# Turns between blocks: ScalarE writes the rounded input itself, and the splits of later weights are moved behind the turning of x

## The chip, the cores and the metric

The kernel runs on one core of one Trainium2 chip. The metric is the device time of that core in microseconds (us). Before the change the median of 3 runs is 1807.88 us (1806.29 to 1808.33). The engines are called PE (matmul; PEld is its weight load), DVE (VectorE), ACT (ScalarE), POOL (GpSimd) and SP (its queue issues most transfers).

## The reference, cut to what matters

A stack of four blocks (gated linear attention, a spatial gating unit, forgetting attention, gated linear attention again) on 256 tokens of 1024 features, followed by a hybrid block (convolution and dilated attention) and a mixture of 16,384 single-vector experts. What matters here is what lies between two blocks:

```
for i in range(DEPTH):                        # 4 blocks
    mod = cond @ w_mod[i] + b_mod[i]          # shift, scale, gate
    h = rms_norm(x, norm_pre_g[i]) * (1.0 + scale) + shift
    o = mixer_i(h)                            # begins with h @ w_in, ends with @ w_out
    x = x + gate * rms_norm(o, norm_post_g[i])
h = x + hybrid_mixer(rms_norm_2(x, norm_mix), ...)
h = h + peer_ffn(rms_norm_2(h, norm_ffn), ...)
return rms_norm_2(h, final_norm)
```

Everything is float32, and the results must hold to nearly that accuracy.

## The kernel before, in words

**Products in three parts.** Every large product a @ w is made of three matmuls in the rounded format fp32r: both operands are split into a high half (the value rounded to fp32r, suffix H or `wh`) and a low half (what the rounding left, suffix L or `wl`), and aH·wh, aH·wl and aL·wh are added up (L420 to L422). A chunk of a weight is 128 x 1024 numbers; `w_load` (L191) brings it in through SP's queue, `w_split` lets ACT write the high half (L200) and DVE the low half (L201), and asks for the load of the chunk four places later. Four raw and six split chunks are kept at a time. `w_next` hands out the next chunk and splits ahead of it; `w_fill(n)` splits all chunks up to number n-1.

**A turn.** x lies with tokens on partitions, and the next block needs h with features on partitions. A turn between two blocks works on the two halves of the tokens, tb = 0 and 1, in turn. The last group of columns of the output product (`proj_tm` with `late`) does its four chunks first for tb 0 and then for tb 1. After tb 0, `consume` takes the sums (square on ACT L348, product with the gate on DVE L484), and `late(0)` works out the norm (L355 to L500), the new x (L505) and the normed x in two pieces of 512 columns, `xn` (L361 in `scaled`). When tb 1's matmuls have been issued, `settle` turns xn of tb 0 with eight PE transposes (L367), and `make_h` works on the result: per 128 features one ACT instruction writes scaled and shifted h (L385, or L383 where there is no shift), and per pair of these DVE copies the rounded high half (L388) and subtracts for the low half (L389). Then `late(1)` begins the same for tb 1, whose turning falls into the first group of the next block (`proj_tm` with `early`), between that group's four chunks for tb 0 and its four for tb 1. There are five such turns: into sgu, fox, the second gla, the hybrid block and the experts' query (L1194 to L1204 work on its result). The first gla has an early group without a turn before it.

**Order.** The kernel is scheduled by hand: each engine runs its instructions in the order in which the program emits them. The table `FILL` tells after which chunk of the first (tb 0) and of the second pass (tb 1) further weights are split. Let `first` be the number of the first chunk of the group. Before the pass begins, chunks up to first+4 are split already. In the late group `w_fill(first+6)` therefore splits one chunk in the first pass, and `w_fill(first+7)` and `w_fill(first+8)` one each after the first and second chunk of the second pass. In the early group that follows, chunks e+0 to e+3 are its own (e = first+4), and its fills split e+4 and e+5 in the first pass and e+6 and e+7 in the second. `consume` comes before `settle` in both passes.

**Beside it.** Generators in `tasks` and `later` advance one step at each `tick`. One of them, `mod_steps`, runs beside each of the four blocks and adds up one chunk of `w_mod` per tick on DVE (L252, L254) for the modulation of later blocks, and asks SP for the chunk after the next (`m_load`, L237). In both gla blocks a long row of DVE work (`decay`, `k_scale`) has to be done before the scores (L652) can begin.

Of the kernel before, what the change touches and what calls it, by code (L numbers as in the profile page):

```python
# [8 lines left out]
F32 = mybir.dt.float32  # L9
# [3 lines left out]
AF = mybir.ActivationFunctionType  # L13
ALU = mybir.AluOpType
# [11 lines left out]
RAW = 4  # L26
HIGH = 6
LEAD = 5
FILL = ((5, 6, 0, 0), (7, 8, 0, 0))
PJ = 3  # L30
RAW2 = 3
HIGH2 = 3
# [29 lines left out]
def _build(ctx, nc, tc, I, out, dbg):  # L62
# [14 lines left out]
    act = nc.scalar.activation  # L77
    tt = nc.vector.tensor_tensor
    ts = nc.vector.tensor_scalar
# [3 lines left out]
    def pj():  # L83
        return ps_j.tile([P, 512], F32, tag="pj", name="pj")
# [13 lines left out]
    def tick():  # L98
        for g in list(tasks):
            try:  # L100
                next(g)
            except StopIteration:
                tasks.remove(g)
        tick_later()
# [5 lines left out]
    def tick_later():  # L110
        for g in list(later):
            try:
                next(g)
            except StopIteration:
                later.remove(g)
        return bool(later)
# [4 lines left out]
    x = keep.tile([P, NTB, D], F32, name="x")  # L121
# [31 lines left out]
    for l in range(4):  # L153
        if l in (0, 3):
            j = l // 3
# [37 lines left out]
    def w_split(i):  # L193
        if i >= len(plan):
            return
        w = raw.pop(i)
        pool = spool if i < first_down else late_pool[0]
        wh = pool.tile([P, CH], F32R, tag="wh", name="wh")
        wl = pool.tile([P, CH], F32R, tag="wl", name="wl")
        act(wh, w, AF.Copy)  # L200
        tt(wl, w, wh.bitcast(F32), op=ALU.subtract)  # L201
        a = plan[i][1]
        parts[i] = (wh.rearrange("p (a b) -> p a b", a=a), wl.rearrange("p (a b) -> p a b", a=a))
        w_load(i + RAW)

    def w_fill(n):
        while nxt_s[0] < n:
            nxt_s[0] += 1
            w_split(nxt_s[0] - 1)

    def w_next(fill=True):
        i = nxt_w[0]
        nxt_w[0] += 1
        if fill:
            w_fill(min(i + LEAD + 1, max(i, first_down) + HIGH2))
        return parts.pop(i)
# [113 lines left out]
    def advance():  # L330

        for g in list(pend):
            if next(g):
                pend.remove(g)
                turning.append(g)

    def settle():
        while pend:
            advance()
        while turning:  # L340
            for _ in turning.pop(0):
                pass

    HALF = [slice(m * 512, (m + 1) * 512) for m in range(2)]
# [12 lines left out]

    def scaled(tb, r):
        xn = [work.tile([P, 512], F32, tag="xn", name="xn", bufs=2) for _ in range(2)]
        for m in range(2):  # L360
            ts(xn[m], x[:, tb, HALF[m]], r, None, op0=ALU.mult)  # L361
        return xn

    def turned(xn):
        p = pm()
        for j in range(4):
            nc.tensor.transpose(p[:, j * P:(j + 1) * P], xn[:, j * P:(j + 1) * P], ident)  # L367
        return p.rearrange("p (j t) -> p j t", j=4)

    def make_h(tb, r, A, B, hs):  # L370

        h, hH, hL = hs
        tsl = slice(tb * P, (tb + 1) * P)
        xn = scaled(tb, r)
        yield True
        ps = [turned(v) for v in xn]
        for m, p in enumerate(ps):
            k4 = slice(4 * m, 4 * m + 4)
            t = h[:, k4, tsl] if h is not None else work.tile([P, 4, P], F32, tag="tl", name="tl", bufs=2)
            for j in range(4):  # L380
                kt = 4 * m + j
                if B is None:
                    act(t[:, j], p[:, j], AF.Copy, scale=A[:, kt:kt + 1])  # L383
                else:
                    act(t[:, j], p[:, j], AF.Identity, scale=A[:, kt:kt + 1], bias=B[:, kt:kt + 1])  # L385
                if j % 2:
                    e = slice(kt - 1, kt + 1)
                    nc.vector.tensor_copy(hH[:, e, tsl], t[:, j - 1:j + 1])  # L388
                    tt(hL[:, e, tsl], t[:, j - 1:j + 1], hH[:, e, tsl].bitcast(F32), op=ALU.subtract)  # L389

    def proj_fm(n, H, L, consume, nk=KT, per_block=False):

# [19 lines left out]
    def proj_tm(n, H, L, consume, early=False, late=None):  # L412


        def part(p, w, c, tb):
            wh, wl = w
            tsl = slice(tb * P, (tb + 1) * P)
            for k in range(2):
                kt = c * 2 + k
                mm(p, H[:, kt, tsl], wh[:, k], start=(kt == 0), stop=False)  # L420
                mm(p, H[:, kt, tsl], wl[:, k], start=False, stop=False)  # L421
                mm(p, L[:, kt, tsl], wh[:, k], start=False, stop=(kt == KT - 1))  # L422

        for gi in range(n):
            if early and gi == 0 or late is not None and gi == n - 1:
                first = nxt_w[0]
                ws = []
                p = pj()
                for c in range(4):
                    ws.append(w_next(False))  # L430
                    part(p, ws[c], c, 0)
                    advance()
                    if FILL[0][c]:
                        w_fill(first + FILL[0][c])
                consume(gi, 0, p)
                settle()
                if late is not None:
                    pend.append(late(0))
                    advance()
                p = pj()  # L440
                for c in range(4):
                    part(p, ws[c], c, 1)
                    advance()
                    if FILL[1][c]:
                        w_fill(first + FILL[1][c])
                    tick()
                consume(gi, 1, p)
                if late is not None:
                    settle()
                    pend.append(late(1))  # L450
                    advance()
                continue
            ps = [pj() for _ in range(NTB)]
            for c in range(4):
                w = w_next()
                for tb in range(NTB):
                    part(ps[tb], w, c, tb)
                if c == 3:
                    for tb in range(NTB):
                        consume(gi, tb, ps[tb])  # L460
                tick()

    def out_proj(oH, oL, lp, tags, l, A, B, full):
# [30 lines left out]
        def late(tb):  # L494
            r = inv_rms(ss[tb], "a")
            products(1, tb)
            c = tiny.tile([P, 2], F32, tag="c", name="c")
            tt(c, ss[tb][:, 2:6:2], ss[tb][:, 3:6:2], op=ALU.add)
            stt(c[:, 0:1], c[:, 0:1], r, c[:, 1:2], op0=ALU.mult, op1=ALU.add)
            stt(ms[tb], c[:, 0:1], r, ms[tb], op0=ALU.mult, op1=ALU.add)  # L500
            r2 = power(ms[tb], 1, "b")
            yield
            for m in range(2):
                xv = x[:, tb, HALF[m]]
                stt(xv, t[tb][:, HALF[m]], r, xv, op0=ALU.mult, op1=ALU.add)  # L505
            yield from make_h(tb, r2, A(), B(), hs)

        add(gate())
        proj_tm(2, oH, oL, consume, late=late)
        return hs  # L510

# [43 lines left out]
    def gla(l, hs, lp, nA, nB, nF):  # L555
# [63 lines left out]
        def c_v(g, tb, p):  # L619
            if tb == 1:  # L620
                act(v[:, tb, g * 512:(g + 1) * 512], p, AF.Copy)
            else:
                nc.vector.tensor_copy(v[:, tb, g * 512:(g + 1) * 512], p)  # L623

        proj_tm(2, hH, hL, c_v, early=True)

        def c_q(c, p):
# [86 lines left out]
    def sgu(l, hs, lp, nA, nB, nF):  # L714
# [19 lines left out]

        add(mod_steps([1] * 24), later)
        proj_tm(2, hH, hL, c_v, early=True)

        def ln():
# [193 lines left out]
    def hybrid(hs):  # L932
        h, hH, hL = hs
        with tc.tile_pool(name="hyb", bufs=1) as lp:
# [216 lines left out]
            def late(tb):  # L1151
                r = inv_rms(ss[tb], "b")
                yield
                yield from make_h(tb, r, col("norm_ffn", 0, 8), None, hs2)
# [317 lines left out]
    h, hH, hL = hs  # L1472

    def start():
        ss = [tiny.tile([P, 2], F32, tag=f"ss{tb}", name="ss") for tb in range(NTB)]
        for tb in range(NTB):
            for m in range(2):
                square_sum(x[:, tb, HALF[m]], ss[tb][:, m:m + 1])
        yield
        r = [inv_rms(ss[tb], "b", ms[tb]) for tb in range(NTB)]  # L1480
        yield
        for tb in range(NTB):
            xn = scaled(tb, r[tb])
            yield
            for m in range(2):
                d = h[:, 4 * m:4 * m + 4, tb * P:(tb + 1) * P]
                if m:
                    nc.vector.tensor_copy(d, turned(xn[m]))
                else:
                    act(d, turned(xn[m]), AF.Copy)  # L1490
# [155 lines left out]
```

## Time and profile before

| | |
|---|---|
| median of 3 runs | 1807.88 us |
| the profiled execution's own time | 1805.22 us |
| its span | 1803.3 us |
| PE busy (share of the span) | 1689.9 us (94%) |
| DVE busy | 1285.0 us (71%) |
| ACT busy | 970.6 us (54%) |
| chain that ended last, by engine | PE 74%, DVE 13%, ACT 5%, DMA 4%, issue 3% |
| mean granted clock of the core, as a share of full speed | 0.978 |

All rows come from the one profiled execution. A busy time counts an instruction from start to end; where instructions overlap, a row with several (x8) gives the time from the first start to the last end. "idle before" is the engine's idle time just before a group, and the releaser is what ended it.

### The profile page before, as it was taken

How to read it: one execution, taken by the hardware profiler on the slowest of the kernel's cores; microseconds unless marked ns; L12 is line 12 of the kernel's file. 1: busy time of each engine (PE TensorE's matmuls, PEld its weight loads, DVE VectorE, ACT ScalarE, POOL GpSimd, SP SyncE). 2: the span in 40 equal slices, each digit the busy share in tenths (PEclk: the TensorE clock that was granted, in tenths of full speed). 3: DMA queues.
4: the chain of work that ended last, by engine and by line, in shares of the span. 5: the costliest groups of instructions: out<-in, count | busy, mean ns of one | idle time of the engine just before them, and what ended most of it. 6: DMA issues, size and time to landing. Idle time of an engine off the chain costs nothing.

```text
span 1803.3 us, 28515 instructions
## 1 busy us (share of the span) xinstructions
PE 1689.9 (94%) x10774; PEld 1491.9 (83%) x10774; DVE 1285.0 (71%) x2593; ACT 970.6 (54%) x1527; POOL 62.1 (3%) x102
## 2 busy tenths in 40 slices
PE   3989899999989999989988999999999899999997
PEld 2877787777789788879978999999999788888886
DVE  7878787876786756574566889997774466666665
ACT  3535446545545543435353446668894455555554
POOL 0000000000000000000000000000000000000000
PEclk9989999999989999999999999999999899999999
DMA  8765885862553565335553676664447677777774
GB/s 332 268 221 177 294 285 177 314 214 71 169 190 115 190 181 174 114 95 173 170 173 117 203 220 192 204 184 158 156 150 233 199 232 238 236 236 236 236 234 159
DMA packets 104188, 357.08 MB, mean 198 GB/s; under 512 B 12273, under 2 KB 13297, under 8 KB 103794
## 3 DMA queue, kind: packets, MB, share of 16 engines
q1 hardware_dynamic: 97200, 335.52, 58.9%
q0 software_dynamic: 5120, 16.78, 2.4%
q10 hardware_dynamic: 1730, 2.96, 0.5%
q8 instruction: 85, 1.39, 0.3%
q14 instruction: 53, 0.43, 0.1%
HBM read 337.38 MB, written 17.83 MB: 197 GB/s over the span
## 4 chain that ended last, share of the span: by engine, by line
PE 74%; DVE 13%; ACT 5%; DMA 4%; issue 3%; POOL 0%; SPq 0%; DVEq 0%; ACTq 0%; POOLq 0%
PE pm L1433 20%; PE pj L1382 6%; PE pj L1383 6%; PE pj L1381 6%; PE pj L420 5%; PE pj L421 4%; PE pj L422 4%; DVE wl L201 4%; PE pj L403 4%; PE pj L404 4%; PE pj L405 4%; DMA wmod<-in_w_mod 3%; PE pm L1324 3%; DVE macc L254 2%; ACT wh L200 1%
## 5 line engine op out<-in xcount | busy, mean ns | idle before, releaser
L201 DVE TENSOR_TENSOR wl<-wr,wh 128x1024 fp32r<-128x1024 f32 x504 | 613.8, 1222 | 313.8 <-ACT wh L200 312.9
L200 ACT ACTIVATE wh<-wr 128x1024 fp32r<-128x1024 f32 x504 | 527.2, 1054 | 223.3 <-PE pm L1433 52.2
L1381 PE MATMUL pj<-uH,wh 128*128 128x256 f32 x1024 | 293.7, 287 | 0.0
L1382 PE MATMUL pj<-uH,wl 128*128 128x256 f32 x1024 | 289.9, 283 | 0.0
L1383 PE MATMUL pj<-uL,wh 128*128 128x256 f32 x1024 | 289.9, 283 | 0.0
L403 PE MATMUL pj<-hH,wh 128*128 128x256 f32 x768 | 227.0, 296 | 0.3 <-DVE v L623 0.3
L404 PE MATMUL pj<-hH,wl 128*128 128x256 f32 x768 | 221.9, 289 | 2.5 <-DVE wl L201 2.5
L405 PE MATMUL pj<-hL,wh 128*128 128x256 f32 x768 | 221.0, 288 | 0.0
L1382 PEld LDWEIGHTS pj<-uH,wl 128*128 128x128 f32 x1024 | 196.4, 192 | 0.3 <-DVE wl L201 0.2
L1381 PEld LDWEIGHTS pj<-uH,wh 128*128 128x128 f32 x1024 | 196.6, 192 | 0.0
L1383 PEld LDWEIGHTS pj<-uL,wh 128*128 128x128 f32 x1024 | 196.2, 192 | 0.0
L1433 PE MATMUL pm<-wh 128*128 128x512 f32 x512 | 161.6, 397 | 8.1 <-ACT wh L321 8.1
L420 PE MATMUL pj<-wh,hH 128*128 128x512 f32 x352 | 145.1, 412 | 21.0 <-DVE hH L388 16.3
L1433 PE MATMUL pm<-wh,wl 128*128 128x512 f32 x512 | 161.3, 396 | 0.0
L1433 PE MATMUL pm<-wl,wh 128*128 128x512 f32 x512 | 161.3, 396 | 0.0
L403 PEld LDWEIGHTS pj<-hH,wh 128*128 128x128 f32 x768 | 151.6, 197 | 11.5 <-issue 8.3
L404 PEld LDWEIGHTS pj<-hH,wl 128*128 128x128 f32 x768 | 151.8, 198 | 3.4 <-DVE wl L201 3.2
L405 PEld LDWEIGHTS pj<-hL,wh 128*128 128x128 f32 x768 | 151.5, 197 | 0.0
L422 PE MATMUL pj<-wh,hL 128*128 128x512 f32 x352 | 141.7, 403 | 0.3 <-DVE hL L1513 0.3
L421 PE MATMUL pj<-wl,hH 128*128 128x512 f32 x352 | 141.5, 402 | 0.0
L1433 PEld LDWEIGHTS pm<-wh 128*128 128x128 f32 x512 | 97.0, 190 | 31.0 <-ACT wh L321 8.3
L254 DVE SCALAR_TENSOR_TENSOR macc<-wmod,sc,macc 128x1024 f32<-128x1024 f32 x76 | 97.2, 1278 | 32.1 <-DMA wmod<-in_w_mod 31.9
(337 smaller groups left out, 2678.4 us busy)
## 6 DMA issues: line engine op xcount, KB each, us to landing
wr<-in_down SPq DMA_DIRECT2D x128, 512.0 KB, 3.7
wr<-in_up SPq DMA_DIRECT2D x128, 512.0 KB, 4.3
wmod<-in_w_mod SPq DMA_DIRECT2D x88, 512.0 KB, 5.5
wr<-in_hyb_fm SPq DMA_DIRECT2D x40, 512.0 KB, 3.6
wr<-in_hyb_qkv SPq DMA_DIRECT2D x36, 512.0 KB, 3.7
spill<-st POOLq DMA_DIRECT2D x64, 256.0 KB, 3.3
a<-spill SPq DMA_DIRECT2D x64, 256.0 KB, 3.3
wr<-in_fox_qkv SPq DMA_DIRECT2D x24, 512.0 KB, 4.3
```

What stands on the lines that cost most here:

```text
L200: act(wh, w, AF.Copy)
L201: tt(wl, w, wh.bitcast(F32), op=ALU.subtract)
L403: mm(o, wh[:, kt, cs], H[:, kt], start=(kt == 0), stop=False)
L404: mm(o, wl[:, kt, cs], H[:, kt], start=False, stop=False)
L405: mm(o, wh[:, kt, cs], L[:, kt], start=False, stop=(kt == nk - 1))
L420: mm(p, H[:, kt, tsl], wh[:, k], start=(kt == 0), stop=False)
L421: mm(p, H[:, kt, tsl], wl[:, k], start=False, stop=False)
L422: mm(p, L[:, kt, tsl], wh[:, k], start=False, stop=(kt == KT - 1))
L1381: mm(o, wh[:, kt], uH[:, kt], start=(kt == 0), stop=False)
L1382: mm(o, wl[:, kt], uH[:, kt], start=False, stop=False)
L1383: mm(o, wh[:, kt], uL[:, kt], start=False, stop=(kt == KT - 1))
L1433: mm(acc[tb][n], lw[:, m, tsl], ru[:, 0, HALF[n]], start=(i == 0 and lw is wh and ru is uh), stop=(i == P - 1 and lw is wl))
```

## The change

It has four parts. (1) In `scaled` the second of the two pieces of xn is written by ACT. (2) In `make_h` ACT writes the rounded half of each pair of features directly from the turned x, two instructions, and then the unrounded h, two more; DVE's copy is gone and its subtraction stays. (3) `FILL` becomes a table for early and late groups: the late group splits first+5 and first+6 in its passes and first+7 only after `late(1)` has been begun ("end"); the early group splits nothing in its first pass and one chunk after each chunk of the second. (4) `settle` comes before `consume` in both passes.

```diff
-FILL = ((5, 6, 0, 0), (7, 8, 0, 0))
+FILL = {"early": ((0, 0, 0, 0), (5, 6, 7, 8)), "late": ((5, 6, 0, 0), (7, 0, 0, 0)), "end": 8}
...
     def scaled(tb, r):
         xn = [work.tile([P, 512], F32, tag="xn", name="xn", bufs=2) for _ in range(2)]
-        for m in range(2):
-            ts(xn[m], x[:, tb, HALF[m]], r, None, op0=ALU.mult)
+        ts(xn[0], x[:, tb, HALF[0]], r, None, op0=ALU.mult)
+        act(xn[1], x[:, tb, HALF[1]], AF.Copy, scale=r[:, 0:1])
         return xn
...
-            for j in range(4):
+            for j in (0, 2):
                 kt = 4 * m + j
-                if B is None:
-                    act(t[:, j], p[:, j], AF.Copy, scale=A[:, kt:kt + 1])
-                else:
-                    act(t[:, j], p[:, j], AF.Identity, scale=A[:, kt:kt + 1], bias=B[:, kt:kt + 1])
-                if j % 2:
-                    e = slice(kt - 1, kt + 1)
-                    nc.vector.tensor_copy(hH[:, e, tsl], t[:, j - 1:j + 1])
-                    tt(hL[:, e, tsl], t[:, j - 1:j + 1], hH[:, e, tsl].bitcast(F32), op=ALU.subtract)
+                e = slice(kt, kt + 2)
+                for d in (hH[:, e, tsl], t[:, j:j + 2]):
+                    for i in range(2):
+                        k = kt + i
+                        if B is None:
+                            act(d[:, i], p[:, j + i], AF.Copy, scale=A[:, k:k + 1])
+                        else:
+                            act(d[:, i], p[:, j + i], AF.Identity, scale=A[:, k:k + 1], bias=B[:, k:k + 1])
+                tt(hL[:, e, tsl], t[:, j:j + 2], hH[:, e, tsl].bitcast(F32), op=ALU.subtract)
...
             if early and gi == 0 or late is not None and gi == n - 1:
                 first = nxt_w[0]
+                last = late is not None and gi == n - 1
+                fill = FILL["late" if last else "early"]
...
                 for c in range(4):
                     ws.append(w_next(False))
                     part(p, ws[c], c, 0)
                     advance()
-                    if FILL[0][c]:
-                        w_fill(first + FILL[0][c])
+                    if fill[0][c]:
+                        w_fill(first + fill[0][c])
+                settle()
                 consume(gi, 0, p)
-                settle()
...
                 for c in range(4):
                     part(p, ws[c], c, 1)
                     advance()
-                    if FILL[1][c]:
-                        w_fill(first + FILL[1][c])
+                    if fill[1][c]:
+                        w_fill(first + fill[1][c])
                     tick()
+                settle()
                 consume(gi, 1, p)
                 if late is not None:
-                    settle()
                     pend.append(late(1))
                     advance()
+                if last:
+                    w_fill(first + FILL["end"])
                 continue
```

## Rows read from the trace of the kernel before

**Rows 1.** Waits of PE over the span: engine, line, releaser: total, times, longest.

```profile
PE pm L367 <- DVE xn L361: 21.2, 3, 19.8
PE pj L420 <- DVE hH L388: 16.3, 10, 2.4
PE pm L652 <- DVE qk L628: 15.5, 2, 10.2
```

**Rows 2.** Timeline, turn into sgu, tb 0: start, duration, engine, line, operation [idle before].

```profile
166.72 1.41 DVE L505 SCALAR_TENSOR_TENSOR x<-t,rr,x 128x512 f32<-128x512 f32 x2
...
168.84 2.35 DVE L201 TENSOR_TENSOR wl<-wr,wh 128x1024 fp32r<-128x1024 f32 x2
...
169.10 1.04 PE L367 MATMUL pm<-ident,xn 128*128 128x128 f32 x8
169.36 0.60 ACT L348 ACTIVATE jk<-pj 128x512 f32<-128x512 f32 x1 [1.55 <-PE pj L422]
...
169.94 2.89 ACT L385 ACTIVATE tl<-pm,modc 128x128 f32<-128x128 f32 x8
171.10 0.68 DVE L484 TENSOR_TENSOR t<-pj,gate 128x512 f32<-128x512 f32 x1
171.71 0.28 DVE L388 CAST hH<-tl 128x256 fp32r<-128x256 f32 x1
172.02 0.42 DVE L389 TENSOR_TENSOR hL<-tl,hH 128x256 fp32r<-128x256 f32 x1
...
172.04 0.57 PE L420 MATMUL pj<-wh,hH 128*128 128x512 f32 x1 [1.91 <-DVE hH L388]
```

**Rows 3.** Costliest groups of instructions (the page's part 5): ACT's split.

```profile
L200 ACT ACTIVATE wh<-wr 128x1024 fp32r<-128x1024 f32 x504 | 527.2, 1054 | 223.3 <-PE pm L1433 52.2
```

**Rows 4.** Timeline, the same turn, tb 1.

```profile
174.35 0.21 DVE L355 TENSOR_SCALAR v<-ss 128x1 f32<-128x1 f32 x1
...
177.32 0.87 DVE L361 TENSOR_SCALAR xn<-x,rr 128x512 f32<-128x512 f32 x2
...
179.24 1.03 PE L367 MATMUL pm<-ident,xn 128*128 128x128 f32 x8
...
181.20 0.50 PE L420 MATMUL pj<-wh,hH 128*128 128x512 f32 x1 [0.93 <-DVE hH L388]
```

**Rows 5.** Timeline of PE, sgu: chunk e+8 of the weights.

```profile
199.98 0.38 PE L404 MATMUL pj<-hH,wl 128*128 128x256 f32 x1 [2.06 <-DVE wl L201]
```

**Rows 6.** Timeline, tb 1 of the turns into fox, gla and the hybrid block.

```profile
304.37 0.50 PE L420 MATMUL pj<-wh,hH 128*128 128x512 f32 x1 [1.32 <-DVE hH L388]
...
482.60 0.52 PE L420 MATMUL pj<-wh,hH 128*128 128x512 f32 x1 [2.36 <-DVE hH L388]
...
606.28 2.17 ACT L383 ACTIVATE tl<-pm,cols 128x128 f32<-128x128 f32 x8 [0.16 <-PE pm L367]
...
608.40 0.50 PE L420 MATMUL pj<-wh,hH 128*128 128x512 f32 x1 [1.77 <-DVE hH L388]
```

**Rows 7.** Timeline, turn into the experts' query, tb 1.

```profile
930.27 0.60 ACT L1194 ACTIVATE q<-pj 128x512 f32<-128x512 f32 x1 [2.71 <-PE pj L422]
...
933.28 1.04 PE L367 MATMUL pm<-ident,xn 128*128 128x128 f32 x8
...
935.03 0.50 PE L420 MATMUL pj<-wh,hH 128*128 128x512 f32 x1 [0.72 <-DVE hH L388]
```

**Rows 8.** Timeline of SP and DVE, start of the first and second gla.

```profile
46.77 3.53 SPq L191 DMA_DIRECT2D wr<-in_gla_qk  x3
...
57.16 1.28 DVE L254 SCALAR_TENSOR_TENSOR macc<-wmod,sc,macc 128x1024 f32<-128x1024 f32 x1 [4.23 <-DMA wmod<-in_w_mod]
...
496.50 1.28 DVE L254 SCALAR_TENSOR_TENSOR macc<-wmod,sc,macc 128x1024 f32<-128x1024 f32 x1 [2.65 <-DMA wmod<-in_w_mod]
```

**Rows 9.** Stretches just after a restart: PE, PEld, DVE, ACT, POOL busy (x), PEclk, DMA, GB/s.

```profile
172.40:175.80 3.40, 3.40 (x10) 2.63 (x9) 3.02 (x12) 2.94 (x6) 0.93 (x1) 0.51 0.64 218
...
924.70:928.00 3.30, 3.30 (x15) 2.65 (x15) 2.53 (x9) 2.86 (x6) 0.55 (x1) 1.00 0.93 339
```

## The prediction, made before the changed kernel had run

> **What bounds the kernel now.** I read the page first: PE is busy nearly all the time and leads the chain that ended last, so a change pays only where PE stands still. The waits of PE come next [rows 1]: at the ten halves of the five turns it waited 16.3 us in all for DVE's copy of hH, at most 2.4 us at once; of the 21.2 us for xn, 19.8 us are one wait at the start of the kernel. These two rows are all that a better turn could win: about 18 us, 1%. The third row, 15.5 us, is the gla blocks' row of DVE work. Then I read the timeline of one turn [rows 2, 4]. PE has turned xn by 170.14 and starts again at 172.04. ACT's values were there at about 170.4; what came last is DVE, which had two low halves of weights (168.84, 2.35 us) and the gate product L484 ahead of the copy. In tb 1 DVE comes last again, less so (0.93 us).
>
> **The change, step by step, in the turn into sgu.** All times are on the clock of the profiled execution.
>
> *tb 0 starts earlier.* x is ready at 168.13 [rows 2]. ACT writes xn[1] in about 0.6 us (as its 128x512 square L348, 0.60; bounds 0.5, half of the 1024-wide split [rows 3], and 0.9, the two pieces on DVE together [rows 4]), then splits one chunk (1.05 us) and is free at 169.8; the turned values come 0.7 us after the transposes began, also 169.8. PE can start at about 170.35 instead of 172.04: 1.7 us won, and DVE loses the copies and half of xn.
>
> *ACT now sets the pace.* Eight instructions took 2.89 us, 0.36 each [rows 2]; now there are 16, 5.7 us. An instruction that writes hH could cost from 0.28 (DVE's copy of a whole pair) to 0.53 (half of the split's 1.05); I take the same 0.36, the nearest row. The first low half needs four instructions and DVE's 0.42: 171.8. The first pair of features thus waits almost as long as before. From there PE needs 0.22 to 0.23 us per matmul at full clock [rows 9], 1.4 us per pair, and ACT 1.4 us per pair: it keeps up. Three chunks end at 171.8 + 16 x 0.23 = 175.5.
>
> *The fourth weight comes late.* This decides. Chunk e+3 is split only after `late(1)` has begun. Before it on ACT now stand: the 16 instructions (to 175.6), the square of tb 1's sum (0.7 with its read, since `settle` comes first), the wait for DVE's L484 (0.68), the square of t (0.7): the split starts at about 177.4, ends at 178.5, and DVE's low half ends at 179.7. PE needs e+3 at 175.5. It gets one matmul done at 178.5 and waits for the low half until 179.7; tb 0 ends at 180.9. Before, it ended just ahead of 179.24 [rows 4]. The cover that made this split free (it was done during the previous pass) is gone. Bounds for its lateness: 0, if ACT ran the split ahead, which its order excludes, and 4.2 us.
>
> *The chain of tb 1 is later by as much.* Its norm began at 174.35 on DVE behind the hL of tb 0 [rows 4]; now it stands behind 16 ACT instructions, a square and L484: 176.9. The small steps to the new norm take 1.5 us as before, and then e+3's low half (1.2 us, waiting for 178.5) stands in DVE's queue ahead of the new x: it runs from 179.6 to 181.0, xn to 181.4. The transposes start at 181.4 instead of 179.24. After them ACT goes straight to its 16 instructions (first at 182.1): PE starts at 182.65 instead of 181.20, has its first low half at 184.1 and ends tb 1 at 184.1 + 22 x 0.23 = 189.2; before, 181.20 + 24 x 0.23 = 186.8. That is 2.4 us lost.
>
> *The next weights.* e+4 is split after the 16 instructions and `consume` (188.3): its low half ends at 190.55, 1.1 us after PE needs it. Behind it SP's queue waits: the load of raw chunk e+8 needs e+4's buffer, and the third chunk of `w_mod` is asked for behind that, at 190.9. DVE's sum of it stands ahead of e+7's low half, and the fourth ahead of e+8's. At e+8 PE already waited 2.06 us, to 199.98 [rows 5]; I put it at about 204.5. **Turn into sgu: 4.5 us lost** (bounds 2.4, if the `w_mod` chunks land at once, and 6).
>
> *The other turns*, with the same offsets from their transposes and the restarts of [rows 6]. Into fox: end of tb 1 1.75 us later; its DVE is nearly full afterwards, and low halves that come up to 6 us later take up to 3 more from two later waits: 3 taken. Into gla: PE itself only 0.5 us later, as its wait there was the longest (2.36). But the fourth `w_mod` sum (496.50, waiting for its transfer [rows 8]) is asked for 3 us later, and the DVE row behind it, which PE waits for, moves with it: 3. Into the hybrid block: without a shift ACT takes 0.27 each (2.17 for eight), 16 are 4.2 us; 1.1. Into the experts' query: tb 0 loses 2.0 us to the late e+3. Then `settle` goes ahead of `consume`: ACT's copy of q (930.27), on which PE's next transposes and scores wait in order, comes behind 16 ACT instructions. From q's start, 0.2 us after tb 0's pass, to tb 1's transposes were 3.0 us, and to PE's restart 4.76 [rows 7]. Now about 4.75 us go from the transposes' start to the end of ACT's run, then the 3.0 us: 7.8 against 4.96 between the passes, 2.8 more: 4.8 in all (bounds 2, if q overtook, and 6).
>
> *The first gla has no turn, and wins.* With no fill in its first pass the load of one raw chunk (46.77) instead of three (3.53 us, [rows 8]) stands before the `w_mod` transfer for which DVE waited 4.23 us. The sums behind it come up to 3.2 us earlier, and the DVE row that makes PE wait up to 10.2 us with them: 3 won (bounds 0 and 3.2). In the prologue xn[1] on ACT spares DVE 0.9 us, but there DVE waits for PE's transposes: nothing. Loads moved with their splits still have over 10 us, four splits ahead: nothing.
>
> **Sum:** -3 + 4.5 + 3 + 3 + 1.1 + 4.8 = 13.4 us lost. The clock comes on top: after a gap of 1.91 us the granted clock was 0.51 for some 3.4 us, the 1.2 GHz level, with 10 matmuls where 15 were done at 1.00 [rows 9], about 1.1 us each. It happened after three of the ten gaps, and these three are in the times that I compare with; the new gaps of 3 to 4 us in four turns may bring it back, partly under ACT's pace: 1 us. So 14.4 us: the execution of 1805.22 us would take about 1819.6, and the median, 2.7 us above it, 1822.
>
> The page "ScalarE: Activation LUTs" of the Trainium skill (What ACT_TABLE_LOAD costs) gives 0.19 us + 0.83 ns per column, 0.09 for each per-partition operand, and 0.09 of overlap between neighbours. That makes 0.39 per instruction with scale and bias against the row's 0.36; as an estimate of mine from that page, 16 would take 6.2 us instead of 5.7 and the sum would be some 3 to 5 us worse; the trace has the duration, so it stands.
>
> **Rivals.**
> *Faster: the early restart wins.* Its place is the first matmul of each half; its price the 16.3 us of [rows 1] less 0.3 left at each of ten, 13 us, with the first gla's 3: down to 1792. For it speaks that DVE, the late one in each half, loses two copies' worth of work per half; against it that the first low half comes only 0.2 us earlier and e+3 4 us too late. It decides if ACT can begin e+3's split by 174.4, that is if the square and L484 did not lie between.
> *No difference.* The turns lose only what the first gla wins: the 0.5 to 1 us that the other parts cost if the late e+3 is hidden, 1804 to 1811. For it speaks that PE's waits later in the blocks could take up a shift; against it that those waits hang on DVE rows that shift too.
> *Slower still: the clock.* If it falls at every stall of both halves, ten times at 1.1 us and partly twice, with slow transposes, 7 to 10 us come on top: 1829 to 1832. For it speaks that the new gaps are longer than any that made it fall. The page "TensorE: Matmul & The Clock Gate" (HAM oscillation) has the rule that waits between groups of matmuls send the array back to the low clock each time; the trace agrees in three gaps of ten.
> *The change does less than it says*: losses of the weight alone, 4 to 8 us, 1811.5 to 1816, if `w_mod` and the query chain are not on the path.
>
> **How the numbers follow.** A kernel of this length can be told from no change beyond about 0.2%, 3.6 us. Forecast 0.62 (its own range 1816 to 1827); less loss 0.10; slower still 0.14; no difference 0.06; faster 0.08. Slower by over 0.2% is 0.62 + 0.10 + 0.14 = 0.86. The range that leaves out faster, no difference and a third of slower still is 1811.5 to 1831.
>
> **What would show it.** Right: in the turn into sgu PE starts about 1.7 us earlier after the first transposes; then a wait of some 3 us at the fourth chunk for ACT's wh and 1 us for DVE's wl; L201 ahead of L505; tb 1's transposes 2 us later; in the query turn q's copy after 16 L383-like instructions and PE's wait for it over 4 us; in the first gla the wait at L652 down to about 7 us. Wrong: no wait of PE for wh at L420, or e+3's split ahead of the squares on ACT; or xn of tb 1 no later than before.

## The result, and the profile after

The changed kernel took 1829.55 us (median of 4; 1828.32 to 1834.11) against 1808.11 before (median of 4): ratio 1.0125, 95% interval 1.0107 to 1.0144. It is 21.4 us slower. The profiled execution took 1829.79 us, its span is 1827.8 us (before: 1803.3). The wide range (1811.5 to 1831) held the time; the likeliest value, 1822, was 7.5 us short of it, and the forecast's own range (1816 to 1827) missed it. The time lies where the rival "slower still: the clock" was put (1829 to 1832, chance 0.14).

First the waits of PE in the changed kernel, over the span: line, releaser, total, times, longest. The 16.3 us for DVE's hH in ten halves [rows 1] are gone. In their place stand the weight of the fourth chunk (L421 for ACT's L200, five turns, and L422 for DVE's L201), the low halves of h (L423 for hL), and several later waits that were shorter or absent before.

```profile
PE pm L657 <- DVE qk L633: 13.3, 2, 7.5
PE pj L421 <- ACT wh L200: 11.3, 5, 2.8
...
PE pj L423 <- DVE hL L390: 4.8, 8, 0.8
PE pj L422 <- DVE wl L201: 4.6, 7, 0.8
PE pm L1202 <- issue: 4.4, 1, 4.4
...
PE pj L421 <- ACT sq L837: 4.1, 2, 3.7
...
PE pj L404 <- DVE v L628: 1.9, 1, 1.9
...
PE pj L421 <- ACT qk L970: 1.9, 1, 1.9
...
PE pj L405 <- DVE wl L201: 0.4, 1, 0.4
```

The turn into sgu in the changed kernel (start, duration, engine, line; compare [rows 2, 4]). PE restarts 1.21 us after the transposes began instead of 2.94. But ACT writes for 5.5 us (166.32 to 171.79), the square comes after that, the fourth chunk's split only at 173.95, and tb 1's transposes begin 13.02 us after tb 0's instead of 10.14.

```profile
164.74 0.73 ACT L361 ACTIVATE xn<-x,rr 128x512 f32<-128x512 f32 x1 [2.31 <-DVE x L510]
...
165.60 1.03 PE L367 MATMUL pm<-ident,xn 128*128 128x128 f32 x8
...
166.32 0.78 ACT L389 ACTIVATE hH<-pm,modc 128x128 fp32r<-128x128 f32 x2
...
166.81 0.50 PE L421 MATMUL pj<-wh,hH 128*128 128x512 f32 x1 [0.17 <-ACT hH L389]
...
171.79 0.68 ACT L348 ACTIVATE jk<-pj 128x512 f32<-128x512 f32 x1
...
173.95 1.04 ACT L200 ACTIVATE wh<-wr 128x1024 fp32r<-128x1024 f32 x1
...
175.02 1.25 DVE L201 TENSOR_TENSOR wl<-wr,wh 128x1024 fp32r<-128x1024 f32 x1
175.04 0.50 PE L421 MATMUL pj<-wh,hH 128*128 128x512 f32 x1 [2.75 <-ACT wh L200]
...
176.19 1.40 DVE L510 SCALAR_TENSOR_TENSOR x<-t,rr,x 128x512 f32<-128x512 f32 x2
...
178.62 1.91 PE L367 MATMUL pm<-ident,xn 128*128 128x128 f32 x8
```

Next the five stretches from one turn's first transposes to the next (sgu, fox, gla, hybrid, query up to the next block's first product). Columns: stretch, length, then busy time and count of PE, PEld, DVE, ACT and POOL, granted clock, DMA share, GB/s. First the kernel before:

```profile
169.10:291.87 122.77, 115.09 (x695) 99.38 (x694) 96.98 (x140) 60.17 (x103) 5.44 (x5) 0.96 0.73 251
291.87:470.26 178.39, 168.67 (x920) 131.18 (x918) 138.82 (x296) 96.40 (x206) 3.65 (x4) 0.96 0.57 191
470.26:596.77 126.51, 116.79 (x735) 103.22 (x734) 91.31 (x149) 67.18 (x111) 6.24 (x8) 0.95 0.50 162
596.77:921.90 325.13, 314.38 (x2106) 278.03 (x2104) 203.33 (x372) 149.97 (x219) 2.46 (x4) 0.99 0.52 158
921.90:943.84 21.94, 16.75 (x90) 13.07 (x88) 14.07 (x27) 11.91 (x28) 0.55 (x1) 1.00 0.58 190
```

and the changed kernel:

```profile
165.60:291.53 125.93, 117.36 (x696) 99.68 (x695) 94.80 (x129) 67.04 (x122) 5.00 (x5) 0.95 0.71 244
291.53:476.58 185.05, 168.22 (x919) 129.39 (x918) 136.48 (x285) 102.77 (x225) 4.31 (x4) 0.97 0.54 184
476.58:609.10 132.52, 119.99 (x735) 104.76 (x734) 88.95 (x138) 73.87 (x130) 6.90 (x8) 0.92 0.48 154
609.10:938.92 329.82, 317.55 (x2106) 278.52 (x2105) 200.68 (x361) 155.79 (x238) 3.11 (x4) 0.98 0.51 155
938.92:968.12 29.20, 19.82 (x89) 15.11 (x88) 12.74 (x18) 17.69 (x46) 0.55 (x1) 0.88 0.40 132
```

The lengths grew by 3.16, 6.66, 6.01, 4.69 and 7.26 us: 27.8 in all. The first transposes come 3.5 us earlier (165.60 against 169.10 [rows 2]), and the rest after the query is as long as before (859.68 against 859.46 us): -3.5 + 27.8 + 0.2 = 24.5, the difference of the two spans. Now read PE's busy time: with nearly the same number of matmuls (4545, before 4546) it is 742.94 us against 731.68, 11.3 more, nearly all of it in sgu, gla, hybrid and query; in the last three the granted clock fell too (0.95 to 0.92, 0.99 to 0.98, 1.00 to 0.88). So 16.5 of the 27.8 us are idle time of PE, and 11.3 are busy time of matmuls that took longer.

### The profile page after: what moved, and what is told of

It reads as the page before. It is cut to its first block, busy times and chain, and to the rows that moved or that the text cites. A ratio compares the mean times of both kernels' runs of the same rounds, so it can differ in the third digit from the quotient of the medians.

```text
span 1827.8 us, 28544 instructions
## 1 busy us (share of the span) xinstructions
PE 1700.0 (93%) x10774; PEld 1493.9 (82%) x10774; DVE 1272.7 (70%) x2541; ACT 1002.6 (55%) x1619; POOL 63.9 (3%) x102
## 4 chain that ended last, share of the span: by engine, by line
PE 52%; issue 22%; DVE 11%; ACT 7%; DMA 5%; POOL 2%; SPq 0%; ACTq 0%; POOLq 0%; DVEq 0%
PE pm L1438 20%; PE pj L404 4%; PE pj L422 4%; PE pj L423 4%; PE pj L421 4%; PE pj L405 4%; PE pj L406 4%; DVE wl L201 4%; DMA wmod<-in_w_mod 3%; ACT wh L200 2%; POOL spill L1395 2%; DVE macc L254 2%; ACT hH L389 1%; ACT prb L890 1%; PE pj L1388 1%
## 5 line engine op out<-in xcount | busy, mean ns | idle before, releaser
L201 DVE TENSOR_TENSOR wl<-wr,wh 128x1024 fp32r<-128x1024 f32 x504 | 615.4, 1224 | 326.8 <-ACT wh L200 325.8
L200 ACT ACTIVATE wh<-wr 128x1024 fp32r<-128x1024 f32 x504 | 527.5, 1055 | 219.4 <-PE pm L1438 50.9
L404 PE MATMUL pj<-hH,wh 128*128 128x256 f32 x768 | 226.3, 295 | 3.0 <-DVE v L628 1.9
L405 PE MATMUL pj<-hH,wl 128*128 128x256 f32 x768 | 221.2, 288 | 0.5 <-DVE wl L201 0.4
L421 PE MATMUL pj<-wh,hH 128*128 128x512 f32 x352 | 147.2, 418 | 23.3 <-ACT wh L200 11.3
L404 PEld LDWEIGHTS pj<-hH,wh 128*128 128x128 f32 x768 | 151.0, 197 | 14.1 <-issue 7.6
L405 PEld LDWEIGHTS pj<-hH,wl 128*128 128x128 f32 x768 | 151.1, 197 | 1.2 <-DVE wl L201 1.0
L423 PE MATMUL pj<-wh,hL 128*128 128x512 f32 x352 | 143.9, 409 | 5.1 <-DVE hL L390 4.8
L422 PE MATMUL pj<-wl,hH 128*128 128x512 f32 x352 | 143.8, 408 | 4.6 <-DVE wl L201 4.6
L1438 PEld LDWEIGHTS pm<-wl,wh 128*128 128x128 f32 x512 | 97.0, 190 | 22.7
```

The lines of the kernel that those rows point to most:

```text
L404: mm(o, wh[:, kt, cs], H[:, kt], start=(kt == 0), stop=False)
L405: mm(o, wl[:, kt, cs], H[:, kt], start=False, stop=False)
L1438: mm(acc[tb][n], lw[:, m, tsl], ru[:, 0, HALF[n]], start=(i == 0 and lw is wh and ru is uh), stop=(i == P - 1 and lw is wl))
```

## The experiments

Two theories came out of the prediction. A: the fourth weight's late split is the main loss. B: ScalarE's sixteen instructions are, by what stands behind them. Beside them: C, the order of consumer and turning; D, the early groups' moved splits; and later X, that ScalarE waits in order for the new x before it can write xn[1]. Each ratio is to the kernel before, measured beside the run on the same chip.

**e1: the changed kernel with the late groups' splits as before.**

```
-FILL = {..., "late": ((5, 6, 0, 0), (7, 0, 0, 0)), "end": 8}
+FILL = {..., "late": ((5, 6, 0, 0), (7, 8, 0, 0))}
```

> The changed kernel with the late groups' splits put back where they were in the kernel before (5, 6 in the first pass, 7, 8 in the second, none at the end); all else stays changed, the later splits of the early groups too. Theory A (the fourth weight e+3, split only after the norm of tb 1 has begun, is the main loss: its wait of 2.7 us for wh at L421 in three turns and 1.5 to 1.6 in two, 0.76 us more for wl, and the later new x behind it): the waits of L421 for L200 in the turns vanish, tb 1 is turned about 10 to 11 us after tb 0 instead of 13, and 12 to 18 of the 21 us come back: 1810 to 1817 us. Theory B (16 instructions on ScalarE instead of 8 pace everything): the wait for wh goes, but PE then waits for hL or for the new x by as much: 1823 or more. Theory D (the early groups' splits, moved from the first into the second pass, load the stretch behind the turn): no more than 5 us come back: 1824 to 1829.

Measured: 1824.31 us, ratio 1.0089 (1.0067 to 1.0111). Some 5 us came back, far from theory A's 12 to 18. The trace says why. In the turn into sgu (timeline of PE and ACT) the weight's wait is gone, but PE now stands 3.02 us for xn instead of 2.75 for the weight: the square still comes only at 172.01, behind the sixteen.

```profile
172.01 0.69 ACT L348 ACTIVATE jk<-pj 128x512 f32<-128x512 f32 x1
...
176.93 1.92 PE L367 MATMUL pm<-ident,xn 128*128 128x128 f32 x8 [3.02 <-DVE xn L360]
```

Two chains hang on the same run of ACT; shortening one leaves the other. A falls as the main cause; the time fits B, and also the edge of what D allowed (e11 tests D).

**e2: the changed kernel with the consumer ahead of the turning again.**

```
-                settle()
                 consume(gi, 0, p)
+                settle()
...
```

The second pass is changed in the same way.

> The changed kernel with the consumer of a pass ahead of the rest of the turning again, in both passes, as in the kernel before. Theory C (the squares, q's copy and the norm of tb 1 are late because they stand behind ScalarE's 16 instructions): the wait of 4.4 us in the experts' query shrinks to about 2, tb 1 is turned 1 to 2 us earlier in the four other turns, and 6 to 9 us come back: 1821 to 1824 us. Theory A (the late fourth weight decides; the consumer's order is a small part): 2 to 4 us come back, in the query: 1826 to 1828 us. If the squares now hold up ScalarE's values of tb 0, PE waits at a later pair of features and nothing comes back.

Measured: 1825.98 us, ratio 1.0106 (1.0080 to 1.0132): 3 to 4 us back. That is less than theory C's 6 to 9 us and fits the 2 to 4 us that A gave it. In the query the wait of 4.4 us became one of 1.5 us for q, but then PE waited 3.5 us for the sub-keys' transfer (see e12), and the stretch stayed long there (27.6 us, against 29.2).

**e3: the kernel before with ScalarE's part alone** (xn[1], and the 16 instructions; splits and order as before).

```
+        act(xn[1], x[:, tb, HALF[1]], AF.Copy, scale=r[:, 0:1])
...
+                for d in (hH[:, e, tsl], t[:, j:j + 2]):
+                    for i in range(2):
+                        act(d[:, i], p[:, j + i], AF.Identity, ...)
```

> The kernel before with ScalarE's part of the change alone: xn[1] on ScalarE and 16 instructions that write hH and the values directly; all splits and the order as before. Theory A (ScalarE's part is harmless, the split order costs): each half starts 0.7 to 1.7 us earlier, part of which the pace takes back: 1800 to 1810 us. Theory B (ScalarE's 16 instructions set the pace, and with the splits among them they come later still): 3 us lost per turn: 1818 to 1825 us.

Measured: 1830.94 us, ratio 1.0117 (1.0099 to 1.0134). ScalarE's part alone loses as much as the whole change, more than B had expected. No split was moved here.

**e4: the kernel before with the moved splits in the first gla alone.**

```
+FILL = {"early": ((5, 6, 0, 0), (7, 8, 0, 0)), ..., "first": ((0, 0, 0, 0), (5, 6, 7, 8))}
```

> The kernel before with one thing of the change: the four splits in the first gla alone are put into the second pass of the early group (all other early groups, the late groups and ScalarE's work as before). Theory: the w_mod transfer for which VectorE waited 4.2 us is asked for earlier, and the 3.5 us that the first turn's transposes came earlier in the changed kernel stay to the end: 1804 to 1805.5 us. Rival: the earlier start is eaten by a later wait, as the stretch from the first turn on is bound by the transfers of w_mod, which do not come earlier: 1807 to 1809 us.

Measured: 1805.44 us, ratio 0.9985 (0.9973 to 0.9997). The first turn begins 4.0 us earlier (165.07), and 2.6 us of it is still there at the end of the query. The theory holds, though its 0.15% lies at the edge of what can be told.

**e5: the kernel before with the 16 instructions alone**, and **e6: with xn[1] on ScalarE alone.**

```
e5: make_h as changed, scaled() as before
e6: scaled() as changed, make_h as before
```

> The kernel before with one part: ScalarE writes hH and the values itself, 16 instructions per half; xn stays on VectorE, splits and order as before. Theory B1 (the 16 instructions set the pace: in the run with ScalarE's whole part the value instructions of the turn into sgu took 5.6 us per half and VectorE's norm of tb 1 waited for the last of them): 12 to 20 us lost, 1820 to 1828 us. Theory B2 (ScalarE stands still for 2.3 to 2.9 us at xn[1], as it waits in order for the new x, and the splits behind it come late; the 16 instructions alone cost little): 1809 to 1816 us.

> The kernel before with one part: xn[1] on ScalarE; hH stays VectorE's copy, splits and order as before. Theory B1 (the 16 instructions are the cost): 1804 to 1811 us, as the half of xn spared on VectorE pays for the later splits. Theory B2 (ScalarE's wait for x holds up two splits, and with them VectorE's low halves, the hH copies behind those and PE): 0.8 to 1.5 us lost per half in nine halves, 1814 to 1822 us.

Measured: e5 1813.18 us, ratio 1.0021 (1.0010 to 1.0033); e6 1820.51 us, ratio 1.0055 (1.0038 to 1.0073). Here B1 misses and B2 fits both: alone, one instruction moved to ScalarE costs more than eight added there. The timelines show what e6 does: ACT stands 2.31 us at xn[1] of tb 0 until x is there (3.8 to 4.5 us in tb 1 of the first four turns), with two splits behind it, and DVE's low halves and copies of hH follow them; PE restarts 4.05 us after the transposes began, not 2.94.

```profile
167.59 0.72 ACT L361 ACTIVATE xn<-x,rr 128x512 f32<-128x512 f32 x1 [2.31 <-DVE x L507]
168.22 1.99 ACT L200 ACTIVATE wh<-wr 128x1024 fp32r<-128x1024 f32 x2
...
168.46 1.03 PE L367 MATMUL pm<-ident,xn 128*128 128x128 f32 x8
...
172.51 0.50 PE L420 MATMUL pj<-wh,hH 128*128 128x512 f32 x1 [3.02 <-DVE hH L388]
```

The two do not add: 0.21% and 0.55% alone, 1.17% together in e3. The kernel before has a row that can explain it (timeline of ACT, the same turn, end of tb 0's pass): ACT is done with its work there and idles 4.10 us.

```profile
173.29 2.04 ACT L200 ACTIVATE wh<-wr 128x1024 fp32r<-128x1024 f32 x2
179.43 0.60 ACT L733 ACTIVATE v<-pj 128x512 f32<-128x512 f32 x1 [4.10 <-PE pj L422]
```

The eight added instructions take 2.7 us of that; the wait at xn[1] takes 2.3 us in tb 0 and, in e3, 2.9 in tb 1. The sixteen alone find room there, both do not, and e6 loses in another way, by its late restart. That account is argued from these rows and the three times; no run varied the room itself.

**e7: the changed kernel with t written by VectorE from PSUM**, so that ScalarE has 8 instructions per half.

```
-   for d in (hH[:, e, tsl], t[:, j:j + 2]): ...
+   act(hH[:, e, tsl][:, i], p[:, j + i], AF.Identity, ...)
+   ts(t[:, j + i], p[:, j + i], A[:, k:k + 1], B[:, k:k + 1], op0=ALU.mult, op1=ALU.add)
```

> The changed kernel, but the values t are written by VectorE from PSUM (one instruction per 128 columns with scale and shift), so that ScalarE has 8 instructions per half and not 16; all else as changed. Theory B1 (the pace of the 16): ScalarE's run in a half shrinks from 5.6 to about 2.9 us, tb 1 is turned about 2 us sooner after tb 0, q's copy comes 2 to 3 us sooner, and 10 to 16 us come back: 1814 to 1820 us. Rival (the splits and the clock decide, or VectorE's eight new instructions of some 0.2 to 0.3 us take what ScalarE gives): at most 4 us back, 1825 us or more.

Measured: 1852.75 us, ratio 1.0229 (1.0202 to 1.0256). Theory B1 missed. The time falls under the rival's "1825 us or more", but the run does not decide between the two: a new wait, which neither named, swamped it. ACT and DVE now read the same PSUM tile, and their instructions take turns; in the turn into sgu ACT was at its eight from 165.45 to 173.0 us (timeline of ACT; the idle time before six of them ended with DVE's t, 0.48 us in most cases, 1.27 at the longest).

```profile
168.09 0.46 ACT L390 ACTIVATE hH<-pm,modc 128x128 fp32r<-128x128 f32 x1 [0.48 <-DVE tl L391]
```

The page "PSUM — Partial Sum Buffer" of the Trainium skill (PSUM bank collisions raise a hardware error) states that the compiler back end makes two instructions of different engines wait for each other when they touch the same bank and partitions, two reads included; the trace agrees, with mostly 0.48 us of waiting per instruction.

**e8: the kernel before with the late groups' moved split alone.**

```
+FILL = {..., "late": ((5, 6, 0, 0), (7, 0, 0, 0)), "end": 8}
```

> The kernel before with one part: in the late groups the fourth weight of the next block is split after the norm of tb 1 has begun; ScalarE's and VectorE's work in the turning and the early groups' splits as before. Theory A, the step of the forecast that was to decide (PE waits some 3 us per turn for that weight, and tb 1 follows later): with ScalarE's run at 2.9 us the weight is 2.7 us earlier than in the changed kernel, and 4 to 12 us are lost: 1812 to 1820 us. Rival (the weight's lateness is a consequence of ScalarE's run, and alone it is hidden, or pays by what VectorE has less ahead of its hH copies): 1804 to 1810 us.

Measured: 1812.46 us, ratio 1.0015 (0.9999 to 1.0031). By the ratio that is about 2.7 us, between the two expectations and at the edge of what can be told; the median itself lies at the foot of A's 1812 to 1820. The trace says more. With ACT's run at 2.9 us [rows 2] PE has no wait for wh in the turns, and 3.1 us in four waits for wl (L421). The query stretch is 3.0 us longer than before (24.97 against 21.94), and there PE waited 2.8 us for the sub-keys (see e12), not for the weight.

**e9: the changed kernel with xn[1] back on VectorE**, and **e10: with the 16 instructions taken out** (VectorE copies hH again; xn[1], splits and order stay changed).

```
e9:  scaled() as before, all else as changed
e10: make_h as before, all else as changed
```

> The changed kernel with xn[1] back on VectorE; the 16 instructions, splits and order stay changed. Theory B2 (the largest part alone was xn[1], +10 us on the kernel before, as ScalarE waits in order 2.3 to 3 us for the new x with splits behind it; in the changed kernel it costs as much): 8 to 14 us back, 1815 to 1821 us. Rival (the moved splits leave only one split, or none, behind xn[1], so that its wait costs little there, and the loss sits in the 16 instructions ahead of the squares and of e+3's split): at most 4 us back, 1825 to 1829 us.

> The changed kernel with VectorE's copies to hH back, ScalarE with 8 instructions per half; xn[1], splits and order stay changed. Theory B1 (in the changed order everything stands behind ScalarE's 16: the squares, e+3's split, q's copy): ScalarE's run is 2.9 instead of 5.6 us, e+3's split and tb 1 come some 2.5 us sooner in each turn, and 9 to 15 us come back: 1814 to 1820 us. Rival (VectorE's copies, 1.1 us more per half, make the low halves and x later by nearly as much; the 16 alone cost only 4 us on the kernel before): at most 5 us back, 1824 us or more.

Measured: e9 1833.43 us, ratio 1.0145 (1.0125 to 1.0165): nothing comes back, so the rival holds, though the time is above its 1825 to 1829. e10 1807.31 us, ratio 0.9997 (0.9986 to 1.0007): all of it comes back, more than B1 had expected. This run carries the verdict. In the turn into sgu (timeline of e10) PE restarts later than in the changed kernel, 2.32 us after the transposes began, and still tb 1 comes 10.07 us after tb 0, not 13.02: the square stands 3.45 us and the fourth split 5.98 us behind the first transposes, in the changed kernel 6.19 and 8.35. PE's wait for the weight's wh is 0.36 us (the one for wl stays, 0.78).

```profile
165.29 1.03 PE L367 MATMUL pm<-ident,xn 128*128 128x128 f32 x8
...
166.00 2.89 ACT L385 ACTIVATE tl<-pm,modc 128x128 f32<-128x128 f32 x8
...
167.61 0.50 PE L420 MATMUL pj<-wh,hH 128*128 128x512 f32 x1 [1.28 <-DVE hH L388]
...
168.74 0.64 ACT L348 ACTIVATE jk<-pj 128x512 f32<-128x512 f32 x1
...
171.27 1.04 ACT L200 ACTIVATE wh<-wr 128x1024 fp32r<-128x1024 f32 x1
...
172.36 0.50 PE L420 MATMUL pj<-wh,hH 128*128 128x512 f32 x1 [0.36 <-ACT wh L200]
...
175.36 1.10 PE L367 MATMUL pm<-ident,xn 128*128 128x128 f32 x8 [0.29 <-DVE xn L360]
```

Its five stretches show that the longer matmuls go with the gaps: PE's busy time is 731.85 us, that of the kernel before, and the clock in gla is 0.96 (before 0.95). Not every turn comes back: the query is still 3.9 us longer than before, and what the first gla wins covers that.

```profile
165.29:287.30 122.01, 115.58 (x696) 99.29 (x695) 96.67 (x137) 61.50 (x106) 5.00 (x5) 0.96 0.73 252
287.30:466.20 178.90, 167.45 (x919) 129.62 (x918) 138.12 (x293) 98.64 (x209) 4.32 (x4) 0.97 0.57 190
466.20:592.33 126.13, 116.56 (x735) 102.31 (x734) 90.65 (x146) 68.47 (x114) 6.91 (x8) 0.96 0.51 162
592.33:917.64 325.31, 313.60 (x2105) 276.47 (x2104) 202.31 (x369) 151.51 (x222) 3.11 (x4) 0.99 0.51 158
917.64:943.44 25.80, 18.66 (x89) 14.35 (x88) 14.61 (x26) 13.66 (x30) 0.55 (x1) 0.93 0.46 149
```

**e11: the kernel before with the moved splits in all early groups.**

```
+FILL = {"early": ((0, 0, 0, 0), (5, 6, 7, 8)), "late": ((5, 6, 0, 0), (7, 8, 0, 0))}
```

> The kernel before with the splits of all early groups put into the second pass, and nothing else. Theory (in a turn the early group's first pass is where VectorE comes late, and two low halves less there help as the w_mod transfer did in the first gla): 3 to 8 us won, 1800 to 1805 us. Theory D (the splits moved behind the turn make raw loads and w_mod later and lose in the stretch after it what the first gla wins): 1806 to 1814 us.

Measured: 1803.64 us, ratio 0.9969 (0.9949 to 0.9988). D falls: on the kernel before, the moved splits of the early groups cost nothing on the whole, and this run has the lowest median of all; its interval overlaps that of e4. Where it wins beyond e4 is open: its profiled execution has the 3.7 us of the first gla, but gives 4.4 us back in fox and wins 1.9 in gla.

**e12: e10 with the consumer first in the experts' query alone.**

```
-                settle()
+                if n > 1:
+                    settle()
                 consume(gi, 0, p)
+                settle()
```

> The changed kernel with VectorE's copies to hH back (8 instructions on ScalarE per half) and, in the experts' query alone, the consumer ahead of the rest of the turning in the first pass; xn[1] on ScalarE, moved splits and order elsewhere as changed. Theory (with 8 instructions instead of 16 the four other turns already cost 0.8 us less to 0.5 us more than before and the first gla's 3.5 us stay; what was left was the query turn, 3.9 us, with a wait of 2.4 us for q behind ScalarE's values): the query turn falls back to about 22 us, 1803 to 1805 us. Rival (the query's loss comes from the late weight as well, and scores wait for their table in the new order): 1806 to 1808 us.

Measured: 1809.89 us, ratio 1.0002 (0.9989 to 1.0016). The theory missed, and the time is above the rival's 1806 to 1808 too, but the rival's second reason (scores wait for their table) is what the trace shows. q came early, and PE then waited for the sub-keys (waits of PE in the query):

```profile
PE pm L1208 <- DMA skT<-in_sub_keys: 4.1, 1, 4.1
```

SP's queue shows where they come from: their load stands behind raw loads that wait for the late split's buffer (timeline of SP, first the kernel before, then e12). Before, it was asked for 0.6 us after tb 0's transposes (922.52 against 921.90); in e12 8.1 us after them (926.99 against 918.87), in the changed kernel 9.4 us.

```profile
903.83 18.60 SPq L191 DMA_DIRECT2D wr<-in_w_query  x8
922.52 0.38 SPq L1174 DMA_DIRECT2D skT<-in_sub_keys  x1
```

```profile
900.81 26.08 SPq L191 DMA_DIRECT2D wr<-in_w_query  x8
926.99 0.37 SPq L1180 DMA_DIRECT2D skT<-in_sub_keys  x1
```

## Why the prediction was right in sign and short in size

**The first gla** was right: -3 forecast, -3.5 measured, and e4 holds the mechanism by itself. DVE's wait for `w_mod` there, 4.23 us [rows 8], is at most 1.22 us, and the wait at L652 [rows 1] fell from 10.2 to 7.5 us (forecast: about 7).

**The early restart and the pace.** PE's restart came 1.7 us earlier after the transposes, as forecast, and one of the sixteen took 0.34 us (16 in 5.5 us; forecast 0.36). By the prediction's estimate from the page "ScalarE: Activation LUTs" of the Trainium skill (What ACT_TABLE_LOAD costs) it would be 0.39; the rows decide for 0.34.

**The fourth weight: the step that failed.** The text put "This decides" on the late e+3, and forecast its waits well in the turn into sgu (2.75 for wh and 0.78 for wl against 3 and 1; the four terms that lead to its "177.4" add up to 177.7, and the split came 8.35 us after the first transposes, forecast 8.3). But e1 took the lateness away and got back only about 5 us, and e8 added it alone for 2.7. It was a symptom. The prediction did write that the split and the norm of tb 1 both stand behind ACT's sixteen, but it entered the run itself as costless ("it keeps up") and booked the loss to the weight. e10 removed only the sixteen, and the kernel was back at the time of before. "Keeps up" was true of PE's pass over tb 0, and beside the point: what matters is what stands behind the run on ACT.

The sixteen are needed for the loss, but they do not make it alone (e5, 0.21%). One row orders these runs, the square of t (L348), on which the norm of tb 1 waits. In the turn into sgu it starts 3.58 us after the first transposes in the kernel before, 5.35 in e10 and 6.31 in e5; e10 and e5 cost at most 0.21%. It starts 6.76 us after them in e2, 7.66 in e9, 7.70 in e3, 7.72 in the changed kernel and 8.67 in e1, and these lose 0.89 to 1.45%. So a start up to 6.3 us after the transposes found room and one from 6.8 us on did not; what took the room was the wait at xn[1] ahead of the sixteen in e3, and the squares or the split behind them elsewhere. This reading is argued from the order of these runs. It does not give the size of each loss, and e6 (4.97) loses another way.

**xn[1] on ScalarE** was entered as a gain for DVE. That ACT stands at it until x is there, with its splits behind it, was left out: 2.3 us in tb 0 and 2.7 in tb 1 in the changed kernel, 2.3 and 3.8 to 4.5 in e6, where it alone costs 0.55%. In the changed kernel this does not show as a loss of its own (e9), which fits that only one split stands behind it there in tb 0.

**The terms by turn.** Forecast 4.5, 3, 3, 1.1 and 4.8, in all 16.4; measured 3.2, 6.7, 6.0, 4.7 and 7.3, in all 27.8. In sgu the turn cost more: the next group's first product comes 21.59 us after the first transposes, before 17.67, so 3.9 us later and not 2.4. But "the next weights", entered at some 2 us, gave back: PE's wait at e+8, 2.06 us before [rows 5] and forecast to grow, is 0.41 (L405). In gla the turn cost PE 1.9 us and not 0.5 (the same mark, 22.49 against 20.63 us). The `w_mod` chain moved as forecast, only further: the fourth sum starts 31.25 us after the first transposes, before 26.24 [rows 8].

```profile
507.83 1.28 DVE L254 SCALAR_TENSOR_TENSOR macc<-wmod,sc,macc 128x1024 f32<-128x1024 f32 x1 [1.59 <-DMA wmod<-in_w_mod]
```

PE waits on the DVE row behind it at two places, 1.9 us for v (L404; 0.3 before) and 5.9 for qk (L657; 5.3 before), some 2.3 us more for the forecast's 3. In fox and hybrid new waits came later, behind ACT (3.7 us at L837, 1.1 before; 1.9 us at L970, none before). In the query, PE's wait for q was 4.42 us, as forecast. That turn lost 2.1 us in tb 0 (forecast 2.0), 4.0 between the passes (2.8) and 1.2 behind them (nothing).

**The clock, and matmuls after a gap.** The forecast put 1 us on the clock; PE's busy time grew by 11.3. Over the five stretches PE was busy for 53.8 us while the granted clock was at its lower level (0.50, 1.2 GHz), before for 41.7 and in e10 for 35.4. Of the 12.1 us more, a third (10 matmuls where 15 were done, [rows 9]) to a half is time lost, 4 to 6 us, an estimate. So the clock term was mis-sized by 3 to 5 us, and the other 5 to 7 us had no term at all. They are left for matmuls after a gap, which were not counted one by one: such a matmul is busy 0.50 us, as shown above, where the others follow each other 0.23 us apart. The rival "slower still" gave the clock 7 to 10 us; its time came true, its mechanism only in part, and that is luck. Luck too is that PE's idle time grew by 16.5 us, as much as the forecast's turns lose in all: by turn it grew by 0.9, 7.1, 2.8, 1.5 and 4.2 us.

In the query the clock can be seen in two halves of the changed kernel's trace: after 4.42 us of idle time (for which the profile names no releaser, but q was written from 953.82 on) eight scores matmuls took 2.08 us at a granted clock of 0.50, in the next half 1.16.

```profile
953.82 0.71 ACT L1199 ACTIVATE q<-pj 128x512 f32<-128x512 f32 x1
...
954.64 1.09 PE L1202 MATMUL pm<-ident,q 128*128 128x128 f32 x4 [4.42 <-issue]
956.41 2.08 PE L1207 MATMUL pm<-skT,qT 128*128 128x128 f32 x8 [0.69 <-ACT qT L1204]
...
967.21 1.16 PE L1207 MATMUL pm<-skT,qT 128*128 128x128 f32 x8 [0.75 <-ACT qT L1204]
```

## What to carry to other kernels

Work that moves from a busy engine to an idle one is not paid by its share of busy time: DVE was relieved and ACT was far from full, yet the kernel lost 1.25%, because the work was put ahead of what the next half waits for in ACT's order. So for each added instruction list what stands behind it on its engine, and which chains hang on that; when one delay is seen by PE as two waits, a test that removes one wait only uncovers the other, and only taking the common cause away (e10) decides. Adding that cause alone (e5) is the other half of the test: it showed that the sixteen cost little while the order leaves them room. And an instruction put at a point where its engine must wait for its input (xn[1]) costs that wait for all behind it, in a queue of transfers as well (the sub-keys in e12).

## What had not been expected

Edits of this kind did not add: +0.21% and +0.55% alone made +1.17% together, and with the moved splits and the new order the one that costs more alone, xn[1], could be left in for nothing (e10), while the sixteen without it still made 1.45% (e9). Two engines that only read one PSUM tile took turns in e7, mostly at 0.48 us of waiting per instruction, and the run was the slowest of all. And the stretch after the query, which no edit touches, took 859.46, 859.68 and 861.56 us in the profiled executions of before, of the changed kernel and of e10: lengths of the stretches tell more here than two spans do.
